# Neighbouring weight rows per partition, an expert's first chunk ahead of the second product before it, and the last merge by high and low parts

## The chip, the cores and the metric

One core of a Trainium2 chip runs the whole program. The metric is the device time of one execution in microseconds (us). The core's engines run side by side: TensorE (PE, with its weight loads as PEld), VectorE (DVE), ScalarE (ACT), GpSimd (POOL) and SyncE (SP, which here only issues DMAs and reads register values). They meet through semaphores. Sixteen DMA engines move data between HBM and the on-chip memory SBUF; products accumulate in PSUM.

## The reference

A backbone of two layers on 512 latent tokens and 256 context tokens of 1024 channels, all fp32. Each layer is a mixer (normalised and modulated input, one combined input projection, a convolution group and a gated recurrent group, an output projection onto the residual) and then a mixture of experts. The part that the change touches is the mixture, per token:

```python
group = top-1 of 4 groups (router logits)
e1, e2, g1, g2 = top-2 of the group's 8 experts, with gates     # 32 experts in all
a, u = split(h @ w_e_gu[e])          # [1024] x [1024, 1024]
y    = (silu(a) * u) @ w_e_down[e]   # [512]  x [512, 1024]
x   += m5 * (g1 * y[e1] + g2 * y[e2])
```

The expert weights are 6 MiB each, 32 experts, two layers: 384 MiB that have to be read once. Layer 1 needs only the 512 latent tokens, since nothing reads the context after it.

## The kernel before

The class `Backbone` builds the program. Each layer runs its mixer, its output projection, the routing (`route`, from L875) and then `moe` (L1419). Routing sorts the experts by their number of tokens; each rank is given a fixed room of rows, and `order` (L1568) lists the ranks in the order in which they are computed, so that big experts stand between small ones. A room is cut by `units` into blocks of 128, 64 or 32 rows ("kinds"). What doesn't fit goes to extra blocks (`overflow`, L1454), which are skipped at run time when there are none. Three experts (7, 8, 9, the "static" ones) are taken ahead of routing, so that their weights can be loaded earlier.

**Weights.** `load_chunks` (L1150 to 1163) loads an expert by chunks of 1 MiB, each 256 rows of 1024 columns: four for the first product (`w_e_gu`), two for the second (`w_e_down`). The chunk lies in SBUF as [128 partitions, 2 x 1024]. At L1161 the source is rearranged as `"a (k p) f -> p (a k) f"`: partition p gets row p and row 128 + p, two runs of 4 KB. The chunks go into a ring of some 16 slots (2.7 experts); SP issues each load, in the order of the program, once the slot's last reader is done.

**A block.** `gather` (L1188) fetches the block's token rows by an indirect DMA on POOL's queue. Blocks of 64 and 32 rows hold the halves and quarters of their rows side by side in the 128 partitions. `rows_in` transposes 128 x 128 pieces on TensorE (L1205), and DVE copies them out of PSUM (xT, L1207). `gate_up` multiplies by the chunks of `w_e_gu` (L1220 for 128 rows, L1224 for 64 and 32, where parts of the columns take the array's column tiles in turn). `activate` copies the result on ACT (L1244), transposes it on TensorE (L1247), and forms silu times the other half on ACT (L1250) and DVE (L1251, L1252): that is hT. Then comes the second product with the two chunks of `w_e_down`: `down` in layer 0 (L1277 for 128 rows, L1289 for others; scaled by DVE at L1291 and scattered to HBM by L1180) and `down_here` in layer 1 (L1315, L1327), where the results stay on chip: DVE multiplies them by gate and modulation (L1329) into a tile YB.

**The merge of layer 1.** Blocks of one kind fill the 128 partitions of a YB tile. When a group is full, `tokens` writes one-hots OT of its tokens (L1349) and `merge` (L1352) multiplies OT by YB in fp32 and adds the products to the residual X (L1371): for each of four token tiles, 1024 columns in products of up to 512 columns. There are 13 merges. After the last one, `finish` normalises and stores the result (L1547 to L1550).

**Order.** `begin` (L1373) is a block's whole first product, chunk by chunk; `end` (L1392) its activation and second product. `moe` runs, for each expert, load, begin, end. SP follows the program's order; the other engines' order is set when the program is built, by a scheduler that goes by priorities and by the buffers that are free. The PSUM buffers are three of the tag "acc", two "pS", one "pA"; those of one tag are taken in the order of the program.

Of the kernel before, what the change touches and what calls it, by code (L numbers as in the profile page):

```python
# [19 lines left out]
D = 1024  # L20
# [13 lines left out]
class Backbone:  # L34
# [3 lines left out]
    # ---------------------------------------------------------------- set-up  # L38
    def setup(self, consts, tmp, ps, dram, stp):
# [34 lines left out]
        # lower bounds of layer 1: softmax over the two layers, exp(x) = s(x) / s(-x) for x <= 0  # L74
# [17 lines left out]
        # masks of the levels inside a diagonal block of 32: [s (4 blocks), level, t]  # L92
# [13 lines left out]
    def setup_router(self, consts, tmp):  # L106
# [21 lines left out]
        # token less 1024 as a multiple of 32 and the rest  # L128
# [19 lines left out]
        # which half or quarter of a row a partition takes, with the index that means no row  # L148
# [8 lines left out]
        # rows over which a static expert counts, and what breaks ties between the counts  # L157
# [12 lines left out]
        # of each rank: first column of the table and one, room, whole blocks of 64 in the room  # L170
# [27 lines left out]
    # ------------------------------------------------------- adaLN modulation  # L198
    def ada_step(self, l, g, k, st, pool, ps, q, bufs):
        # rows of four n-blocks of 512 columns in the four column tiles; k-block k of the contraction  # L200
# [22 lines left out]
        if g == 2:  # L223
            # the second norm's weight times (1 + scale)
            nc.vector.scalar_tensor_tensor(row[:64], row[:64], 1.0, st["nw"], op0=OP.add, op1=OP.mult)
# [11 lines left out]
    def ada_cols(self, l):  # L237
        # per-channel factor of the normalised input, norm weight times (1 + scale), for both streams
        nc = self.nc
        A = self.modA[l]  # L240
        nc.vector.tensor_scalar_add(A, self.modc[l][1], 1.0)
        nc.vector.tensor_mul(A, A, self.nwcol(l, 0).unsqueeze(2).to_broadcast([128, 8, 2]))

    # ---------------------------------------------------------------- mixer
# [7 lines left out]
    def square(self, x, pool):  # L252
        # reciprocal root mean square of each token, and space for the normalised tokens
# [10 lines left out]
    def modulated(self, l, i, H, src, pool):  # L264
        # high and low parts of token tile i of the transposed input from its normalised transpose
# [19 lines left out]
    def norm_first(self, H, pool, ps):  # L285
        # the first layer's input: normalised and transposed while the modulation is still being loaded
# [15 lines left out]
    def norm_next(self, sq, x, pool, ps):  # L302
        # a token tile of a later layer's input, normalised and transposed
# [8 lines left out]
    def split_w(self, src, pool, nat=False, eng=None):  # L312
        # src [1024, 128] in DRAM -> [128, (high, low), 8, 128], or [256, 512] -> [128, (high, low), 2, 512]
# [11 lines left out]
    def proj_T(self, W, H, ps, ctx=True):  # L325
        # transposed projection of 128 features: (PSUM tile, token range) for each half of the tokens
# [10 lines left out]
    def proj_N(self, W, H, i, ps, group=range(4)):  # L337
        # natural product of token tile i with 512 columns, over the k-pairs in group
# [10 lines left out]
    def gates(self, l, hd, pz, t, d, K2, Dk):  # L349
        # forget factors and keys of one direction from the raw gate  # L350
# [16 lines left out]
    def head(self, l, hd, K2, Q2, Dk, q, Vn, SG, pool, hg, ps):  # L367
        """One head of the recurrent group. The decay products of both directions come by halving: at block size b
        the two blocks of a pair meet through products inside each block, so nothing is ever divided."""
# [48 lines left out]
        # blocks of 64, and the pairs of 64 inside 128  # L418
# [28 lines left out]
        # pairs of 128  # L447
# [12 lines left out]
        # pairs of 256 of the latent tokens  # L460
# [8 lines left out]
        # final states of the context, both directions  # L469
# [15 lines left out]
        # outputs, natural  # L485
# [22 lines left out]
    def conv(self, l, cb, H, YC, CS, wcol, pool, wp, ps):  # L508
        # gated short convolution of 128 channels: horizontal for the first half of the channels, else vertical
# [39 lines left out]
    def squares(self, CS, ps):  # L549
        # sums over the channels of the last block's squares, for each token  # L550
# [14 lines left out]
    def mixer(self, l, ps, st, ms):  # L565
# [10 lines left out]
        with pool("hy", "right") as hy, pool("wp", "right") as wp, pool("sg", "right") as sgp:  # L576
# [16 lines left out]
            with pool("p0", "right") as p0:  # L593
# [10 lines left out]
                else:  # L604
                    W = nat(6, range(2), nc.vector)
                    # the token tiles in stages, one behind the other
# [1107 lines left out]
```

## Time and profile before

| | us |
|---|---|
| median of 3 runs (2028.06 to 2033.73) | 2029.3 |
| span of the profiled execution | 2028.5 |
| TensorE busy in it | 1726.0 (85%) |
| DVE busy | 908.2 (45%) |
| ACT busy | 442.2 (22%) |
| POOL busy | 360.8 (18%) |

HBM reads are 530.95 MB, 270 GB/s over the span; of 190665 DMA packets 183720 are under 8 KB. Layer 0's mixture lies from about 560 to 1110 us and layer 1's from about 1500 us to the end. The busy shares are means over stages with different limits, so the stages have to be read one by one: the windows (busy time by engine in a stretch, with the granted clock of TensorE and the DMA's busy share and rate), then what an engine waits for, then the timeline of single instructions. In a timeline line, the first number is the start, the second the duration of the group, "x16" its instructions, and the bracket the idle time of the engine before it with what ended it.

### The profile page before, as it was taken

Reading aid. Unit: us, or ns where it says so; the run is one execution under the profiler, and the core shown is the slowest. Engines: PE = TensorE matmul, PEld = TensorE weight load, DVE = VectorE, ACT = ScalarE, POOL = GpSimd, SP = SyncE. Lnnn points to the kernel's source line nnn. Section 1 sums busy time; section 2 is a strip of 40 time slices with the busy share of each in tenths; the row PEclk is TensorE's granted clock in tenths of the full one; section 3 lists DMA queues with packets and bytes.
Section 4 is the critical chain, followed back from the end, with each engine's and each line's share of the span. In section 5 each row is a group of like instructions: output and inputs, shape, how many; then the busy total and the mean of one; then the engine's idle time right before and its main releaser. Section 6 shows DMA issues by size and latency. Waiting matters only on the chain. (4 is left out here: it accounts for less than half of the span.)

```text
span 2028.5 us, 33494 instructions
## 1 busy us (share of the span) xinstructions
PE 1726.0 (85%) x13488; PEld 1104.1 (54%) x13488; DVE 908.2 (45%) x2141; ACT 442.2 (22%) x871; POOL 360.8 (18%) x282
## 2 busy tenths in 40 slices
PE   5999899999967888888875899889968888888886
PEld 2766778898843343333322688767754434434343
DVE  4425355635664132222222636666564434435344
ACT  3512223323212122111111533333320000000001
POOL 1501221121122111111110632222211000000000
PEclk8999899999988999989998899999988999999998
DMA  7376552262489988999998322114379979999996
GB/s 271 99 266 209 177 201 82 75 238 81 172 316 378 409 323 345 408 408 407 407 408 318 134 85 62 42 53 168 126 291 352 407 297 407 407 402 391 401 407 262
DMA packets 190665, 542.36 MB, mean 267 GB/s; under 512 B 17393, under 2 KB 66719, under 8 KB 183720
## 3 DMA queue, kind: packets, MB, share of 16 engines
q1 hardware_dynamic: 167304, 466.17, 60.0%
q10 hardware_dynamic: 15040, 55.08, 7.9%
q0 software_dynamic: 8160, 18.90, 2.5%
q8 instruction: 108, 1.77, 0.4%
q14 instruction: 53, 0.43, 0.1%
HBM read 530.95 MB, written 15.96 MB: 270 GB/s over the span
## 5 line engine op out<-in xcount | busy, mean ns | idle before, releaser
L1224 PE MATMUL acc<-w,xT 128*32 128x256 f32 (+1 forms) x3360 | 348.4, 449 | 18.3 <-DVE xT L1207 9.8
L1224 PEld LDWEIGHTS acc<-w,xT 128*32 128x32 f32 (+1 forms) x3360 | 137.3, 120 | 221.0 <-issue 152.8
L322 POOL TENSOR_TENSOR hilo<-raw,hilo 128x1024 fp32r<-128x1024 f32 x64 | 157.4, 2465 | 447.9 <-ACT hilo L319 406.7
L333 PE MATMUL acc<-HA,hilo 128*128 128x384 f32 (+1 forms) x960 | 208.0, 359 | 0.0
L333 PE MATMUL acc<-HB,hilo 128*128 128x384 f32 (+1 forms) x960 | 205.4, 357 | 0.0
L1244 ACT COPY au<-acc 128x256 f32<-128x256 f32 (+1 forms) x69 | 31.1, 452 | 718.9 <-PE acc L1224 676.7
L333 PEld LDWEIGHTS acc<-HA,hilo 128*128 128x128 f32 x960 | 171.0, 192 | 16.4 <-issue 4.2
L333 PEld LDWEIGHTS acc<-HB,hilo 128*128 128x128 f32 x960 | 173.7, 193 | 9.5 <-issue 0.8
L1188 POOL DMA_INDIRECT xb<-h,idx x63 | 65.3, 1036 | 533.3 <-PE pS L1205 495.0
L1289 PE MATMUL acc<-w,hT 128*32 128x256 f32 (+1 forms) x816 | 115.1, 542 | 47.0 <-DVE hT L1252 42.4
L345 PE MATMUL acc<-hilo,HA 128*128 128x512 f32 x504 | 133.0, 416 | 11.8 <-POOL HA L283 5.8
L345 PE MATMUL acc<-hilo,HB 128*128 128x512 f32 x504 | 125.7, 397 | 4.6 <-DVE hilo L322 3.3
L1268 DVE SCALAR_TENSOR_TENSOR au<-w,gt,au 32x256 f32<-32x256 f32 (+2 forms) x102 | 58.6, 577 | 148.7 <-ACT au L1267 146.2
L345 PEld LDWEIGHTS acc<-hilo,HA 128*128 128x128 f32 x504 | 99.0, 201 | 40.7 <-POOL HA L283 7.3
L1327 PE MATMUL acc<-w,hT 128*32 128x256 f32 (+1 forms) x896 | 88.5, 440 | 28.5 <-DVE hT L1252 22.4
L319 ACT CAST hilo<-raw 128x1024 fp32r<-128x1024 f32 x80 | 83.5, 1049 | 124.8 <-PE acc L345 40.8
L345 PEld LDWEIGHTS acc<-hilo,HB 128*128 128x128 f32 x504 | 94.3, 190 | 30.0 <-DVE hilo L322 4.4
L389 DVE TENSOR_TENSOR Q<-Q,Dk 128x256 f32<-128x256 f32 (+1 forms) x144 | 89.7, 651 | 27.5 <-PE pA L464 11.8
L1289 PEld LDWEIGHTS acc<-w,hT 128*32 128x32 f32 (+1 forms) x816 | 40.1, 140 | 108.8 <-issue 52.3
L1180 POOL DMA_INDIRECT yb<-ys,idx x39 | 38.9, 998 | 288.6 <-DVE ys L1291 204.4
L1207 DVE COPY xT<-pS 128x256 f32<-128x256 f32 (+1 forms) x79 | 42.5, 541 | 95.9 <-PE pS L1205 82.0
L384 DVE TENSOR_TENSOR K<-K,Dk 128x768 f32<-128x768 f32 x64 | 72.9, 1139 | 24.1 <-ACT tmp L401 21.1
(369 smaller groups left out, 2173.4 us busy)
## 6 DMA issues: line engine op xcount, KB each, us to landing
w<-in_w_e_gu SPq DMA_DIRECT2D x242, 1024.0 KB
w<-in_w_e_down SPq DMA_DIRECT2D x121, 1024.0 KB
adaw<-in_w_ada ACTq DMA_DIRECT2D x40, 1024.0 KB
raw<-in_w_in SPq DMA_DIRECT2D x64, 512.0 KB
adaw<-in_w_ada SPq DMA_DIRECT2D x8, 1024.0 KB
raw<-in_w_out SPq DMA_DIRECT2D x16, 512.0 KB
HA<-in_w_e_gu SPq DMA_DIRECT2D x6, 1024.0 KB
h<-SG SPq DMA_DIRECT2D x10, 512.0 KB
```

Of the source, the lines that this page charges most:

```text
L319: nc.scalar.copy(W[:, 0], w)
L322: eng.tensor_sub(W[:, 1], w, W[:, 0].bitcast(F32))
L333: nc.tensor.matmul(o, W[:, wi, k, :], H[k // 4][:, k % 4, hi, t], start=k == 0 and wi == hi, stop=k == 7 and wi == 1)
L345: nc.tensor.matmul(pa, H[k // 4][:, k % 4, hi, t], W[k // 2][:, wi, k % 2, :], start=k == ks[0] and wi == hi, stop=k == ks[-1] and hi == 1)
L384: nc.vector.tensor_tensor(half(Kv, TOK, 0, kn, b), half(Kv, TOK, 0, kn, b), vw(Dv, b, [[2 * b, n], [TOK - b, 2], [0, b]]), op=OP.mult)
L389: nc.vector.tensor_tensor(o, o, vw(Dv, (TOK + b) * d, [[2 * b, qn // (2 * b)], [0, b]]), op=OP.mult)
L1188: self.nc.gpsimd.indirect_dma_start(out=xb, out_offset=None, in_=rows, in_offset=bass.IndirectOffsetOnAxis(ap=idx, axis=0), bounds_check=r ...
L1207: nc.vector.tensor_copy(t[:, :n].rearrange("p a b -> p (a b)"), pt[:, :128 * n])
L1224: nc.tensor.matmul(pg[kind * u:kind * u + kind, :w], xT[k], gu[:, k % 2, w * u:w * u + w], start=st, stop=sp)
L1268: nc.vector.scalar_tensor_tensor(ms[pr, :o], self.m5s[pr, 0, c], g0[pr], ms[pr, :o], op0=OP.mult, op1=OP.add)
L1289: nc.tensor.matmul(py[kind * u:kind * u + kind, :w], hT[k], dn[k // 2][:, k % 2, w * u:w * u + w], start=k == 0, stop=k == 3)
L1327: nc.tensor.matmul(py[pr, :w], hT[k], dn[k // 2][:, k % 2, c], start=k == 0, stop=k == 3)
```

## The change

- `load_chunks` gives each partition two neighbouring rows, one run of 8 KB. Row 2p and 2p + 1 of a chunk then lie in partition p, so the transposes read every second column (`every_other`) to bring the other operand into the same order.
- `begin` is cut in two: `start` (gather, transposes, the first product with chunk 0) and the rest (chunks 1 to 3). `end` runs the next expert's `start` between the last activation and the last second product, where `ahead` allows it: in layer 1 where the next expert is a single block of fewer than 128 rows, in layer 0 for all but rank 0; never for the last expert. The last static expert takes part.
- The merge of layer 1 splits YB into a high part in fp32r (ACT) and a low part in fp32r (POOL), by halves of 512 columns; each product becomes two fp32r products that add up in PSUM. OT becomes fp32r. OT and the parts YR are new tiles, YB moves into free space of X.
- `overflow` gives back the list of scatters that it found, where before it left an empty one.
- The space kept for DMA descriptors of GpSimd is set to 8192.

The rest of the diff takes comments away. Its core:

```diff
     def load_chunks(self, e, which, tiles, q=None):
...
-            o = (q or self.nc.sync).dma_start(w, src[i, r:r + 256, :].rearrange("a (k p) f -> p (a k) f", p=128))
+            o = (q or self.nc.sync).dma_start(w, src[i, r:r + 256, :].rearrange("a (p k) f -> p (a k) f", p=128))
...
+    def every_other(self, t, j):
+        c = 256 * (j // 2) + j % 2
+        return t[:, c:c + 255:2]
...
-                nc.tensor.transpose(pt[:, 128 * j:128 * j + 128], xb[:, 128 * (a + j):128 * (a + j) + 128], self.ident)
+                nc.tensor.transpose(pt[:, 128 * j:128 * j + 128], self.every_other(xb, a + j), self.ident)
...
-            nc.tensor.transpose(pt[:, 128 * j:128 * j + 128], au[:, 128 * j:128 * j + 128], self.ident)
+            nc.tensor.transpose(pt[:, 128 * j:128 * j + 128], self.every_other(au, j), self.ident)
...
     def merge(self, kind, ps):
...
+        YR = self.YR
+        for h in range(2):
+            c = slice(512 * h, 512 * h + 512)
+            nc.scalar.copy(YR[:, 0, c], YB[:, c])
+            nc.gpsimd.tensor_sub(YR[:, 1, c], YB[:, c], YR[:, 0, c].bitcast(F32))
...
-                nc.tensor.matmul(pa[c // 512][:, c % 512:c % 512 + n], self.OT[:, c // w, 128 * i:128 * i + 128],
-                                 YB[:, c:c + n], start=True, stop=True)
+                for v in range(2):
+                    nc.tensor.matmul(pa[c // 512][:, c % 512:c % 512 + n], self.OT[:, c // w, 128 * i:128 * i + 128],
+                                     YR[:, v, c:c + n], start=v == 0, stop=v == 1)
...
     def begin(self, w, units, xp, ps):
+        b, rest = self.start(w, units, xp, ps)
+        rest()
+        return b
+
+    def start(self, w, units, xp, ps):
...
-        for c in range(4):
-            for j, u in enumerate(units):
-                self.gate_up(u[0], xT[j], c, w[c], pg[j])
-        return w, units, pg
+        def chunks(cs):
+            for c in cs:
+                for j, u in enumerate(units):
+                    self.gate_up(u[0], xT[j], c, w[c], pg[j])
+
+        chunks((0,))
+        return (w, units, pg), lambda: chunks((1, 2, 3))
+
+    def ahead(self, l, units):
+        if l:
+            return len(units) == 1 and units[0][0] < 128
+        return sum(1 if u[0] < 128 else 2 * (j > 0) for j, u in enumerate(units)) < 3
+
+    def end(self, b, pool, ps, last=False, between=None):
         w, units, pg = b
...
             if j + 1 < len(units):
                 hT.append(act(j + 1))
+            elif between is not None:
+                between()
             self.down(kind, hT[j], w[4:], wi, pool, ps, last)
...
-                self.YB.append(mp.tile([128, D], F32, name=f"YB{i}"))
+                self.YB.append(self.X[:, 4 + i, :])
...
-            self.OT = self.X[:, 4:6, :].rearrange("p a (b t) -> p (a b) t", b=2)
+            self.OT = mp.tile([128, 4, 512], F32R, name="OT")
+            self.YR = mp.tile([128, 2, D], F32R, name="YR")
...
-        for n, r in enumerate(self.order[l]):
-            e = nc.sync.value_load(self.eid[0:1, r:r + 1], min_val=32 * l, max_val=32 * l + 31)
-            w = self.load_expert(e, self.ring())
-            if n == 28:
-                self.overflow(l, xp, mp, ps, ms2)
-            self.end(self.begin(w, self.units(l, r), xp, ps), mp, ps, n == 28)
-            if l:
-                for u in self.units(l, r):
+        for b in stat[:-1]:
+            self.end(b, mp, ps)
+        cur = stat[-1]
+        for n in range(-1, N):
+            nxt = []
+            fits = n + 1 < N - 1 and self.ahead(l, self.units(l, order[n + 1]))
+            self.end(cur, mp, ps, n == N - 1, (lambda: nxt.append(begin(n + 1))) if fits else None)
+            if l and n >= 0:
+                for u in self.units(l, order[n]):
                     left.remove(u[0])
                 flush()
+            if n + 1 == N - 1:
+                load(n + 1)
+                self.overflow(l, xp, mp, ps, ms2)
+            if n + 1 < N:
+                cur, rest = nxt[0] if nxt else begin(n + 1)
+                rest()
```

Here `load(n)` reads the expert's number and issues its six loads once, and `begin(n)` calls it and then `start`.

## Rows read from the trace of the kernel before

**Rows 1.** Windows by stage: us, busy us (instructions) of each engine, PEclk, DMA share, GB/s.

```profile
260.00:263.00 3.00, 3.00 (x19) 3.00 (x18) 0.00 (x0) 0.00 (x0) 0.00 (x0) 1.00 1.01 423
417.00:435.00 18.00, 18.00 (x101) 18.00 (x101) 5.51 (x67) 3.89 (x6) 3.04 (x2) 0.91 1.02 418
624.00:796.00 172.00, 152.06 (x868) 64.35 (x868) 47.39 (x89) 29.84 (x57) 27.34 (x28) 0.95 0.92 362
796.00:1074.00 278.00, 227.76 (x1706) 92.12 (x1698) 77.00 (x156) 55.74 (x110) 43.35 (x43) 0.92 1.03 407
1559.00:1662.00 103.00, 90.00 (x534) 40.67 (x534) 45.05 (x125) 4.97 (x12) 4.99 (x5) 0.97 0.90 356
1662.00:1990.00 328.00, 280.03 (x2372) 132.23 (x2376) 139.16 (x375) 19.10 (x50) 22.95 (x23) 0.98 1.02 402
1990.00:2004.00 14.00, 8.40 (x113) 4.20 (x106) 7.55 (x39) 1.02 (x3) 0.00 (x0) 0.88 1.00 397
```

**Rows 2.** Waits of TensorE, 796 to 1073 us: total us, times, longest us.

```profile
PE acc L1289 <- DVE hT L1252: 25.0, 12, 2.6
PE pS L1247 <- ACT au L1244: 9.3, 15, 0.7
```

**Rows 3.** Timeline of TensorE, 1073 to 1084 us: start, us, instruction, [idle before].

```profile
1074.55 1.94 PE L1224 MATMUL acc<-w,xT 128*64 128x512 f32 x8 [1.41 <-DMA w<-in_w_e_gu]
```

**Rows 4.** Waits of TensorE, 1662 to 1990 us.

```profile
PE acc L1327 <- DVE hT L1252: 17.9, 15, 1.4
```

**Rows 5.** DMA packets, 260 to 263 us.

```profile
DMA packets 171, 1.27 MB, mean 423 GB/s; under 512 B 16, under 2 KB 16, under 8 KB 16
```

**Rows 6.** Line 410 by form: min/median/max ns, first and last start.

```profile
L410 PE MATMUL pS<-Q,tmp x1600: 189/196/260, 169.1 to 1379.4; 128*32 128x32 f32 x178
...
L410 PE MATMUL pS<-q,tmp x320: 192/196/217, 167.8 to 1363.0; 128*32 128x32 f32 x160
```

**Rows 7.** Timeline of TensorE, 636 to 680 us.

```profile
639.06 5.34 PE L1289 MATMUL acc<-w,hT 128*64 128x512 f32 x16 [2.55 <-DVE hT L1252]
644.33 3.66 PE L1224 MATMUL acc<-w,xT 128*32 128x256 f32 x64
...
653.13 7.09 PE L1224 MATMUL acc<-w,xT 128*64 128x512 f32 x32
660.96 0.66 PE L1247 MATMUL pS<-ident,au 128*128 128x128 f32 x4 [0.74 <-ACT au L1244]
...
664.38 6.32 PE L1289 MATMUL acc<-w,hT 128*64 128x512 f32 x16 [2.55 <-DVE hT L1252]
```

**Rows 8.** Waits of TensorE, 624 to 796 us.

```profile
PE acc L1289 <- DVE hT L1252: 12.5, 6, 2.6
...
PE acc L1224 <- DVE xT L1207: 1.5, 2, 0.8
```

**Rows 9.** Timeline, 1952 to 1964 us, a merge.

```profile
1952.36 1.88 PE L1367 MATMUL pA<-YB,X 128*128 128x512 f32 x4
...
1954.28 1.29 DVE L1371 TENSOR_TENSOR X<-pA,X 128x512 f32<-128x512 f32 x2 [0.17 <-PE pA L1367]
```

**Rows 10.** Timeline, 1993 to 2029 us, the last merge.

```profile
2008.14 1.07 PE L1327 MATMUL acc<-w,hT 128*32 128x256 f32 x16
...
2009.82 0.70 PE L1367 MATMUL pA<-xw,X 128*128 128x256 f32 x2 [0.62 <-DVE xw L1329]
...
2012.09 1.89 PE L1367 MATMUL acc<-xw,X 128*128 128x256 f32 x8
```

**Rows 11.** Timeline of TensorE near 271 and 499 us: fp32r products.

```profile
271.81 2.24 PE L333 MATMUL acc<-HB,hilo 128*128 128x384 f32 x12
...
498.71 21.02 PE L345 MATMUL acc<-hilo,HA 128*128 128x512 f32 x92
```

**Rows 12.** Lines 282 and 283 by form: min/median/max ns.

```profile
L282 ACT CAST HB<-mod x6: 614/617/622, 1130.8 to 1159.4; 128x512 fp32r<-128x512 f32 x6
...
L283 POOL TENSOR_TENSOR HB<-mod,HB x12: 1280/1290/2255, 50.9 to 1160.8; 128x512 fp32r<-128x512 f32 x12
```

More of the change, by code (lines that the diff above doesn't have):

```diff
@@ L1237, in activate @@
             for j in range(4):
-                nc.tensor.transpose(pt[:, 128 * j:128 * j + 128], h[:, 128 * j:128 * j + 128], self.ident)
+                nc.tensor.transpose(pt[:, 128 * j:128 * j + 128], self.every_other(h, j), self.ident)
             nc.scalar.copy(hT.rearrange("p a b -> p (a b)"), pt)
@@ L1386, in begin @@
                 pg.append([ps.tile([128, 512], F32, name="acc", bufs=3) for _ in range(2)])
-        for c in range(4):
-            for j, u in enumerate(units):
-                self.gate_up(u[0], xT[j], c, w[c], pg[j])
-        return w, units, pg
-    def end(self, b, pool, ps, last=False):
+        def chunks(cs):
[9 more added lines that the diff above has]
+    def end(self, b, pool, ps, last=False, between=None):
         w, units, pg = b
@@ L1425, in moe @@
             for i in range(2):
-                self.YB.append(mp.tile([128, D], F32, name=f"YB{i}"))
+                self.YB.append(self.X[:, 4 + i, :])
                 nc.gpsimd.memset(self.YB[-1], 0.0)
-            self.OT = self.X[:, 4:6, :].rearrange("p a (b t) -> p (a b) t", b=2)
+            self.OT = mp.tile([128, 4, 512], F32R, name="OT")
+            self.YR = mp.tile([128, 2, D], F32R, name="YR")
             self.groups, self.into = {}, {}
-        for b in stat:
-            self.end(b, mp, ps)
         left = [u[0] for r in self.order[l] for u in self.units(l, r)]
@@ L1439, in flush, with load, begin @@
                     self.merge(kind, ps)
-        for n, r in enumerate(self.order[l]):
-            e = nc.sync.value_load(self.eid[0:1, r:r + 1], min_val=32 * l, max_val=32 * l + 31)
-            w = self.load_expert(e, self.ring())
-            if n == 28:
-                self.overflow(l, xp, mp, ps, ms2)
-            self.end(self.begin(w, self.units(l, r), xp, ps), mp, ps, n == 28)
-            if l:
-                for u in self.units(l, r):
+        order = self.order[l]
+        ws = {}
+        def load(n):
+            if n not in ws:
+                r = order[n]
+                e = nc.sync.value_load(self.eid[0:1, r:r + 1], min_val=32 * l, max_val=32 * l + 31)
+                ws[n] = self.load_expert(e, self.ring())
+        def begin(n):
+            load(n)
+            return self.start(ws[n], self.units(l, order[n]), xp, ps)
+        N = len(order)
+        for b in stat[:-1]:
[7 more added lines that the diff above has]
+                for u in self.units(l, order[n]):
                     left.remove(u[0])
                 flush()
+            if n + 1 == N - 1:
[4 more added lines that the diff above has]
+                rest()
     def overflow(self, l, xp, mp, ps, ms2):
@@ L1456, in overflow @@
         NOV = self.NOV
+        scats = self.scats
         _, vals = nc.values_load_multi_w_load_instructions(self.nov[0:1, 0:1], min_val=0, max_val=NOV)
@@ L1522, in overflow @@
                     self.merge(64, ps)
-        self.scats = []
+        self.scats = scats
     def combine(self, l, i, cp):
@@ L1701 @@
     from concourse.bass_utils import run_bass_kernel_spmd as _run
-    nc = _bacc.Bacc("TRN2", target_bir_lowering=False, num_devices=1)
+    nc = _bacc.Bacc("TRN2", target_bir_lowering=False, num_devices=1, dynamic_dma_scratch_size=8192)
     arrays, io = {}, {}
```

## The prediction

> **What bounds the kernel now.** I read the windows by stage first, then what TensorE waits for, then its timeline at single boundaries between experts, and last the end of the run. The two layers' expert stages are nearly all weight traffic: from 796 us to 1074 us and from 1662 us to 1990 us the DMA engines show a busy share above 1 and a flat 407 and 402 GB/s [rows 1]. In a stretch like that the end is set by two things only: when the stretch began, and the rate. Each stretch begins where TensorE has caught up enough to free the ring of weight chunks: ahead of them the mean is 362 GB/s (624 to 796 us) and 356 GB/s (1559 to 1662 us) [rows 1], because the big experts there occupy TensorE longer than their weights take to load. So the kernel is bound twice over, first by TensorE and then by DMA.
>
> It isn't DMA alone, though. In 796 to 1073 us TensorE never waits for a weight; it waits 25.0 us in 12 places for the activation of its own first product, and 9.3 us in 15 places for the copy ahead of it [rows 2]. It runs into weights that have not landed only at 1074.55 us [rows 3]. The TensorE chain, its own gaps included, is as long as the transfers. **A faster transfer therefore pays only if that chain becomes shorter too, and the reverse**; both are touched here. In layer 1 it is alike: 17.9 us in 15 waits for the activation [rows 4]. The profiled span is 2028.5 us and the median 2029.3 us, 0.8 us above it; I sum against the span and add the 0.8 at the end.
>
> **Part 1, one run of 8 KB per partition instead of two of 4 KB.** It touches the 32 x 6 chunks of 1 MiB of each layer, at line 1161. The price is the rate per full busy share. 4 KB loads with little else beside them moved 418 GB/s at a share of 1.02, so 410; the adaLN weights, whose rows give 8 KB runs (155 of the 171 packets are not under 8 KB [rows 5]), moved 423 at 1.01, so 419 [rows 1]. That is 2.2%. The lower end is the plain ratio, 423 to 418 or 1.2%. The upper end is against the ring's own stretch, 402 in place of 423 or 5.2%; it counts the short gather packets of those stretches as if the change removed them, so I stay near the like-for-like row and take 2.6%, a little above it, since the ring's packets take longer than those. The saturated stretches are 796 to 1082 us and 1662 to 2003 us, 286 and 341 us: 2.6% is **7.4 and 8.9 us** (3.4 to 14.9 and 4.1 to 17.7).
>
> By the Trainium skill ("DMA: Bandwidth & Descriptors", section "Why small descriptors are slow (HBM only)") a packet carries a fixed overhead of about 3 cycles beside one per 32 bytes, and joining packets is worth it only at 256 bytes or less. As an estimate from that page, 131 cycles twice against 259 is 1.15%, 7 us for both layers in place of 16; the ratio of the rows goes above that, and no run of before moves expert weights in 8 KB runs.
>
> **Part 2, transposes that read every second column.** The number and size of the transposes stays; only the stride of what they read changes. The nearest pair are the small products of one head, with a plain and with a strided operand: median 196 ns both, 106 to 113 ns for the weight load both [rows 6]. I put it at 0; four transposes take 0.66 us [rows 7], so if the stride cost a tenth, the 380 would cost 6 us, the other end.
>
> **Part 3, the next expert's chunk 0 ahead of the second product.** At a boundary TensorE ends the first product, transposes, and stands until DVE has made hT: 2.55 us at 639.06 and at 664.38 us [rows 7]. A quarter of the next first product now fits there: 0.9 us for a block of 32 rows (64 instructions in 3.66 us), 1.8 us for one of 64 (32 in 7.09 us) [rows 7]. In 624 to 796 us there are six such waits, 12.5 us together, and two for xT, 1.5 us [rows 8]. One of the six stands before rank 0 and isn't filled. The rest take 0.9 three times, and 1.8 twice, and the xT waits go: 2.7 + 3.6 + 1.5 = 7.8 us. The second product after a gap is also slow: 5.34 and 6.32 us [rows 7] where 16 at the pace of 32 in 7.09 us [rows 7] would be 3.55, so 1.8 and 2.8 lost to the lower of the two clock levels. I count half of that, 2.3 us. Sum **10 us** (3 if only the waits before 32-row experts go, 14 if every wait listed does). It moves the start of the saturated stretch, and so the end of layer 0, one for one. Inside that stretch the chain gains 12 boundaries at 0.9 to 1.8 us, some 16 us, against the 7.4 that the faster weights ask of it; so both move together. In layer 1 the same in 1559 to 1662 us: five boundaries, one of 1.8 and four of 0.9, 5.4 us. Inside the saturated stretch, 15 waits of 17.9 us [rows 4] give back some 13, enough for 8.9. Of what moves with it: the gather of the next block, one DMA on POOL's queue, is asked for earlier on a queue with slack; the weight loads on SP keep their order, and each waits as before for its slot.
>
> **Part 4, the last layer's merge.** Before, a merge of a 64- or 128-row group is 16 instructions of 512 columns (four in 1.88 us [rows 9]), one of a 32-row group 32 of 256 (eight in 1.89 us [rows 10]): 7.5 us either way, two passes for each fp32 product. After, the two passes are fp32r products: 92 of 512 columns took 21.02 us, 0.23 each, and twelve of 384 took 2.24, 0.19 each [rows 11]; the weight loads set that pace, so I take it for 256 too. 16 x 0.23 = 3.7 us, 32 x 0.19 = 6.0 us: 3.8 and 1.5 less. New is a lead-in: for each half ACT writes the high part (0.62 us) and POOL the low part (1.29 us in the median, 2.26 at most) [rows 12]. The first half is ready after 1.9 us, the second after 3.2. Then DVE's eight additions, 0.64 us each (two in 1.29 [rows 9]), are the floor, 5.2 us in all: the last additions end some 0.6 + 2 x 1.3 + 0.5 + 6 x 0.65 = 7.6 us after the group is full, where the products alone took 7.5 before. Unfilled a merge is thus about the same length (up to -1.3, lost); filled with the next expert's chunks up to +2. Waiting behind POOL's subtractions on its queue are only gathers that are asked for early, and ACT's copies stand ahead of an activation by 0.6 us. I take 0 for the merges inside the stretch, and -1.4 in all for the three ahead of 1662 us, which leaves **4 us** of the 5.4. At the very end nothing fills it: the last merge now begins 0.62 us after the first scaling [rows 10] and chases the others; behind the parts it can't. **-1.6** (to -2.8).
>
> **The rest.** The weights of layer 1 come at 397 GB/s until 2004 us [rows 1], and the last second product uses the last of them at 2008.14 [rows 10], about 4 us later; a chain shortened by part 3 takes that back: **+4** (0 if it isn't). Scatters no longer ordered behind the overflow's, and the smaller descriptor space: 0, as nothing waits for them.
>
> **Sum.** Layer 0: 10 + 7.4 = 17.4. Layer 1: 4 + 8.9 + 4 - 1.6 = 15.3. 2028.5 - 32.7 + 0.8 = **1997 us**, rounded up.
>
> **The rivals.** (a) *The longer packets bring only 1.2%*, the plain ratio of [rows 1]: 627 us x 1.2% = 7.5 in place of 16.3, **2004 us**. The Trainium skill's rule on packets would give about the same. (b) *The rate stays*, since the bound of a saturated stretch is elsewhere than in the packets: only 10 + 4 - 1.6 and the 4 at the end remain, **2013 us**. Against it stands that two kinds of stretch, both saturated, differ in rate [rows 1]. (c) *The chain isn't shortened*: the order of the engines puts chunk 0 behind the second product, as the accumulators in use block it, or the lower clock stays; then TensorE is the bound of both stretches and the faster weights are hidden: 3 us at most, **2025 us**. For it: TensorE runs into missing weights only at 1074.55 [rows 3]. (d) *Slower: the merge's lead-in.* If POOL's subtractions take their longest, 2.26 us [rows 12], a merge ends 0.6 + 4.5 + 0.5 + 3.9 = 9.5 us after its group is full in place of 7.5 and a little, and DVE's scaling of the next block stands behind its additions: with 2.7 us at 13 merges, 35 us, against the 18 that part 3 gives back in layer 1, and 1.6 at the tail, layer 1 gets 19 us longer; layer 0 gains 10 (one of its two parts): **2038 us**. It decides from the point where the lead-in is longer than the TensorE work that stands ready beside it. Against it: the median of 1.29 [rows 12], and that chunks of the next expert can stand there.
>
> **How the numbers follow.** Forecast 0.55, by itself 1981 to 2009. (a) 0.15, (b) 0.08, (c) 0.11, (d) 0.11. Adding the ends of the unknown costs (all waits closed and 5.2% gives 1977 or so), the range that holds eight in ten reaches from 1977 to 2022. A measurement of this kernel tells about 0.3%, 6 us, from no change; so faster is the forecast, (a) and (b), 0.78; (c) is mostly within, 0.10; (d) is slower, 0.12.
>
> **What would show it.** After: the queue of the weights has some 49 thousand packets fewer, and 98 thousand fewer are under 8 KB; 418 to 420 GB/s in the saturated stretches; groups of 8 or 16 first products ahead of a second product in TensorE's timeline, with waits for hT nearly gone; the stretch of layer 0 starts near 786 us; TensorE waits for weights earlier than 1074 us; each merge behind a copy on ACT and a subtraction on POOL. If the rate stays below 410, part 1 is wrong; if the second products still follow idle time of 2 us, part 3 is; if the merges idle TensorE by more than 3 us each, (d) holds.

## The result, and the profile after

| | us |
|---|---|
| before, median in the first comparison (2028.06 to 2033.73, 4 runs) | 2030.97 |
| changed, median (1996.05 to 2005.23, 4 runs) | 1998.14 |
| ratio, with its 95% interval | 0.9844 (0.9822 to 0.9865) |
| changed, median in a second comparison (5 runs; before 2029.48, 11 runs) | 1998.96 |
| its ratio | 0.9843 (0.9815 to 0.9870) |
| span of the profiled execution, before and after | 2028.5 and 1994.8 |

The forecast was 1997 us. The page of the changed kernel counts the packets:

```profile
DMA packets 141513, 542.35 MB, mean 272 GB/s; under 512 B 17394, under 2 KB 66720, under 8 KB 85417
```

That is 49152 packets fewer in all and 98303 fewer under 8 KB (183720 before): 384 chunks, each with 128 packets in place of 256. The stages of the changed kernel by windows (columns as in [rows 1]); the first two lines are layer 0's saturated stretch and its end, the other two layer 1's:

```profile
784.00:1052.00 268.00, 223.93 (x1622) 93.65 (x1622) 74.80 (x155) 54.41 (x108) 42.89 (x41) 0.93 1.01 417
1052.00:1068.00 16.00, 11.55 (x70) 4.20 (x72) 2.77 (x5) 2.41 (x4) 0.99 (x1) 0.82 1.01 418
...
1636.00:1950.00 314.00, 266.90 (x2346) 127.39 (x2338) 146.04 (x386) 30.25 (x68) 45.80 (x41) 0.98 1.01 416
1950.00:1960.00 10.00, 4.19 (x52) 1.88 (x52) 3.60 (x19) 0.65 (x2) 0.00 (x0) 1.00 1.02 419
```

The rate is 417 and 416 GB/s where it was 407 and 402 [rows 1]. TensorE's waits show whose turn it is now, first in layer 0 ahead of the saturated stretch (610 to 784 us, which answers to [rows 8]):

```profile
PE acc L1230 <- DVE xT L1213: 6.5, 7, 1.5
...
PE acc L1295 <- DVE hT L1258: 1.7, 1, 1.7
```

and then inside it (784 to 1056 us, which answers to [rows 2]):

```profile
PE acc L1230 <- DMA w<-in_w_e_gu: 14.3, 5, 5.5
```

The waits for hT have all but gone, from 12.5 us to 1.7 us and from 25.0 us to nothing, and TensorE waits for weights: 14.3 us, where it waited for none before. The transfers alone are the bound there now. What took the place of a wait for hT is a wait for xT, the next block's own rows. The timeline of TensorE, to be held against [rows 7]:

```profile
626.05 0.75 PE L1253 MATMUL pS<-ident,au 128*128 128x128 f32 x4 [0.69 <-ACT au L1250]
626.64 0.40 PE L1211 MATMUL pS<-ident,xb 128*128 128x128 f32 x2
627.91 1.07 PE L1230 MATMUL acc<-w,xT 128*32 128x256 f32 x16 [0.87 <-DVE xT L1213]
629.69 3.65 PE L1295 MATMUL acc<-w,hT 128*64 128x512 f32 x16 [0.71 <-issue]
...
639.11 3.00 PE L1230 MATMUL acc<-w,xT 128*64 128x512 f32 x8 [1.51 <-DVE xT L1213]
642.05 2.50 PE L1295 MATMUL acc<-w,hT 128*32 128x256 f32 x32
```

Ahead of the second product at 629.69 us stand 1.07 us of the next expert's chunk 0, but they begin 0.87 us late, since DVE ends a scaling first and copies xT, from 627.44 us, among the steps of hT. At 639.11 us the wait for xT is 1.51 us, eight instructions take 3.00 us where the warm pace is 1.94 [rows 3], and the second product behind them 2.50 where 1.93 is warm.

### The profile page after: what moved, and what is told of

Its sections match the earlier page's. It is cut to its first block, busy times and chain, and to the rows that moved or that the text cites. A ratio compares the mean times of both kernels' runs of the same rounds, so it can differ in the third digit from the quotient of the medians.

```text
span 1994.8 us, 33498 instructions
## 1 busy us (share of the span) xinstructions
PE 1700.2 (85%) x13488; PEld 1098.2 (55%) x13488; DVE 914.0 (46%) x2141; ACT 458.2 (23%) x897; POOL 394.3 (20%) x308
## 5 line engine op out<-in xcount | busy, mean ns | idle before, releaser
L1230 PE MATMUL acc<-w,xT 128*32 128x256 f32 (+1 forms) x3360 | 378.4, 454 | 59.1 <-DVE xT L1213 34.6
L345 PEld LDWEIGHTS acc<-hilo,HB 128*128 128x128 f32 x504 | 94.5, 190 | 29.1 <-DVE hilo L322 4.5
L1295 PE MATMUL acc<-w,hT 128*32 128x256 f32 (+1 forms) x816 | 97.2, 478 | 12.4 <-DVE hT L1258 6.4
L389 DVE TENSOR_TENSOR Q<-Q,Dk 128x256 f32<-128x256 f32 (+1 forms) x144 | 89.6, 651 | 23.7 <-PE pA L464 11.8
L1333 PE MATMUL acc<-w,hT 128*32 128x256 f32 (+1 forms) x896 | 87.4, 440 | 7.3 <-DVE hT L1258 5.2
L1297 DVE TENSOR_TENSOR ys<-acc,au 128x256 f32<-128x256 f32 (+1 forms) x34 | 18.4, 542 | 124.9 <-PE acc L1295 124.5
```

Source lines behind the costliest of these rows:

```text
L345: nc.tensor.matmul(pa, H[k // 4][:, k % 4, hi, t], W[k // 2][:, wi, k % 2, :], start=k == ks[0] and wi == hi, stop=k == ks[-1] and hi == 1)
L389: nc.vector.tensor_tensor(o, o, vw(Dv, (TOK + b) * d, [[2 * b, qn // (2 * b)], [0, b]]), op=OP.mult)
L1230: nc.tensor.matmul(pg[kind * u:kind * u + kind, :w], xT[k], gu[:, k % 2, w * u:w * u + w], start=st, stop=sp)
L1295: nc.tensor.matmul(py[kind * u:kind * u + kind, :w], hT[k], dn[k // 2][:, k % 2, w * u:w * u + w], start=k == 0, stop=k == 3)
L1333: nc.tensor.matmul(py[pr, :w], hT[k], dn[k // 2][:, k % 2, c], start=k == 0, stop=k == 3)
```

## The experiments

One table for all of them. It is read off the profiles by a ruler that doesn't depend on where a wait is booked: the time at which a given weight chunk had landed, counted back over the bytes of the weight queue. "Start" is from the issue of one given load (in layer 0 the third routed expert's second, in layer 1 the first routed expert's third) to the landing of the chunk that opens the saturated stretch. "Stretch" is 102 chunks in layer 0 and 114 in layer 1, and the chunk that closes it is the fifth and the ninth before the layer's last. "Rest" ends with the layer's last second product, "end" is from there to the end of the span, and "else" is all of the span that is left: mixers, routing, the first experts. Each line adds up to the span of its profile. Every variant is made from the changed kernel and keeps its loop and its `overflow`; `a_alone`, `c_alone` and both `no_d` have the old descriptor space as well, and no run changes that space by itself.

```
us                       layer 0: start stretch  rest   layer 1: start stretch  rest   end    else
before                            181.4   275.8  21.8            153.9   303.1  28.5  19.3  1044.7
a_alone                           181.4   269.7  21.6            155.1   306.7  33.4  19.4  1037.1
c_alone                           176.0   275.5  23.6            153.4   299.1  30.1  19.4  1044.6
d_alone                           180.7   275.7  21.9            152.5   300.1  32.5  20.7  1044.8
no_c                              183.2   269.3  23.2            155.4   302.9  34.0  21.7  1047.0
no_d                              178.6   269.0  23.4            155.5   292.0  29.5  19.4  1043.8
no_d_b                            174.6   269.1  23.5            151.8   292.1  28.9  19.4  1049.4
no_a                              173.2   275.5  23.6            150.7   299.4  29.6  21.0  1044.5
changed, first profile            176.9   269.1  23.2            148.5   292.1  29.1  20.7  1035.2
after_again                       177.7   269.2  23.5            149.5   292.1  29.1  20.7  1043.5
after_b                           174.0   269.3  23.8            148.5   292.1  29.1  20.8  1041.7
plain                             177.1   269.1  22.7            149.4   292.0  29.2  21.0  1044.7
plain_tail                        173.9   268.9  23.4            149.4   292.0  29.2  19.3  1047.1
short_runs                        180.3   291.3  20.7            154.5   318.1  29.2  20.0  1052.0
```

The stretches repeat to within a few tenths of a microsecond wherever the transfers are the bound. The starts scatter by some 4 us, and "else", where no kernel but `plain` and `plain_tail` changes an instruction of the mixers, scatters by more than 10 us. The chunk that bounds a stretch is met to within some half a chunk, so that a start can be 1 to 2 us too long, and its rest as much too short (`a_alone`, `d_alone` and `no_c` above all).

**8 KB runs alone (a_alone).** The kernel before with

```diff
-            ...rearrange("a (k p) f -> p (a k) f", p=128))
+            ...rearrange("a (p k) f -> p (a k) f", p=128))
```

and the transposes to match.

> The kernel before with 8 KB runs and the strided transposes alone. My theory (TensorE's chain is as long as the transfers): the saturated stretches show some 417 GB/s at first, but the ring then runs against TensorE, the mean rate there falls back towards 410, and the time is 0 to 6 us below before (2024 to 2030). Rival (the gains simply add): the rate alone gives its 2.5% over 627 us, 15 us less, about 2015. If the strided transposes cost a tenth each: some 3 us above my theory.

Measured: ratio 1.0009 (0.9984 to 1.0034), median 2030.83 against 2032.38. Nothing is left of 2.4% of the rate. The windows of the two stretches:

```profile
796.00:1070.00 274.00, 225.29 (x1677) 93.83 (x1677) 77.04 (x156) 54.83 (x109) 43.35 (x42) 0.95 1.01 417
1653.00:1976.00 323.00, 277.79 (x2180) 131.50 (x2180) 134.22 (x356) 18.43 (x48) 22.95 (x23) 0.96 0.98 399
```

In layer 0 the rate is there, 417 GB/s, and the stretch is 6.1 us shorter. In layer 1 the DMA share falls to 0.98 and the rate to 399: the ring waits for TensorE, and the stretch and the rest behind it are 3.6 and 4.9 us longer. So the gain of one layer is lost in the other. That TensorE is late there shows at the end: by the bytes of the queue, the last weights had landed 11.3 us before the last second product ended in `a_alone` and 11.8 us in `no_c`, and 3.2 us in before. TensorE's mean granted clock differs with it: 0.95 and 0.96 in the two stretches here, 0.92 and 0.98 before [rows 1]. Where TensorE is the bound, such dips are time; what makes them differ is open. `no_c`, which has the new merge as well, shows the same.

**Chunk 0 ahead, alone (c_alone).** The changed kernel with the runs of 4 KB, plain transposes and the fp32 merge, in effect the kernel before with `start`, `end`, `ahead` and the new `overflow`.

> The kernel before with the next expert's chunk 0 ahead of the second product alone; runs of 4 KB, the old merge. My theory: the saturated stretches start 5 to 10 us earlier in each layer, their rate stays 407 GB/s, TensorE waits for weights before their end: 10 to 16 us below before (2014 to 2020). Rival (the chain isn't what counts, the rate is): within 4 us of before.

Measured: ratio 0.9948 (0.9929 to 0.9967), median 2023.07: 9 to 11 us less, at the lower end of what I expected. Windows of the stretches, and what TensorE waits for in the second one:

```profile
788.00:1060.00 272.00, 221.35 (x1621) 89.19 (x1621) 72.23 (x148) 53.38 (x106) 43.31 (x41) 0.92 1.03 407
1659.00:1980.00 321.00, 280.80 (x2311) 128.13 (x2308) 138.14 (x364) 19.00 (x50) 22.95 (x23) 0.99 1.03 407
```

```profile
PE acc L1229 <- DMA w<-in_w_e_gu: 7.3, 3, 5.5
```

The rate is that of 4 KB runs, 407 GB/s, and now in both layers; before, layer 1 had 402. The 114 chunks take 299.1 us in place of 303.1: before, TensorE had held up the transfers of layer 1 by 4 us, unseen, since the share stood at 1.02. Layer 0's stretch starts 5.4 us earlier, layer 1's only 0.5, where I had expected 5 to 10 us in each.

**The merge alone (d_alone).** The changed kernel with `return False` in `ahead`, 4 KB runs and plain transposes.

> The kernel before with the merge by high and low parts alone. My theory: the lead-in of copy and subtraction eats what the cheaper products save, so within 4 us of before (2026 to 2034). Rival (the lead-in is unfilled at each of 13 merges, 2 to 3 us each): 10 us or more above before. Rival on the other side (the merge is what moved layer 1's stretch by 9 us in the changed kernel): 6 to 9 us below before.

Measured: ratio 0.9988 (0.9968 to 1.0008). No change that can be told, as my theory said; the end is 1.4 us longer, and the rest of layer 1 by 4.0, against 4.4 less ahead of it.

**Without chunk 0 (no_c).** The changed kernel with

```diff
     def ahead(self, l, units):
+        return False
```

> The changed kernel without chunk 0 ahead (8 KB runs and the new merge stay). My theory: near the time of 8 KB runs alone, 2020 to 2030, as the chain binds. Rival (gains add): 2012 or less.

Measured: ratio 0.9992 (0.9972 to 1.0011). The runs of 8 KB and the merge together are worth nothing that can be told without the chunk ahead. By the medians the parts alone give 1.6, 9.3 and 1.9 us, 13 us, of which only the 9.3 is clear of the scatter; the whole is 31 to 33 us. The difference is what the parts give each other. For the merge it can be read from TensorE's waits for the two parts, over the whole run; here:

```profile
PE pA L1379 <- ACT YR L1369: 20.6, 13, 1.8
PE pA L1379 <- POOL YR L1370: 9.3, 13, 0.9
```

and in the changed kernel:

```profile
PE pA L1379 <- POOL YR L1370: 9.7, 17, 0.9
PE pA L1379 <- ACT YR L1369: 7.0, 7, 1.8
```

That is 2.3 us a merge without chunk 0 ahead and 1.3 us with it.

**Without the merge (no_d, no_d_b).** The changed kernel with

```diff
-                for v in range(2):
-                    nc.tensor.matmul(..., self.OT[...], YR[:, v, c:c + n], start=v == 0, stop=v == 1)
+                nc.tensor.matmul(..., self.OT[...], YB[:, c:c + n], start=True, stop=True)
```

OT and YB where they were before, and the descriptor space as before.

> The changed kernel with the old fp32 merge. My theory (the merge is worth about nothing in the stretch and costs 2 us at the end): 1995 to 2000, the same as the changed kernel. Rival (the cheaper products are what let the chain of layer 1 keep up): 2004 or more.

Measured: ratio 0.9891 (0.9859 to 0.9923), median 2009.98: not what I expected, and what the rival said. It was run again beside the changed kernel on one chip:

> The changed kernel with the old fp32 merge again, beside the changed kernel. The profiles so far put the new merge's worth at 6 to 7 us in layer 1's stretch with chunk 0 ahead, less 1.4 us at the end: 4 to 7 us above the changed kernel. If that was the scatter of single runs: the same within 2 us.

Measured: ratio 0.9891 (0.9862 to 0.9920) and median 2009.6, where the changed kernel (`after_b`) has 0.9843 and 1998.96. The medians are 10.6 us apart, and both runs of `no_d` agree. The stages account for a part: layer 1's start is 151.8 and 155.5 us here, 148.5 to 149.5 in the changed kernel, so 2 to 7 us, less 1.4 at the end. The rest of the difference lies in "else" in these profiles (1049.4 against 1041.7), where the two kernels differ only in the space kept for descriptors and in where YB and OT lie; why the medians keep it is open, and a part of the 10.6 us may belong to that and not to the merge. How the merge pays is seen at the 128-row group, one of three ahead of layer 1's stretch. TensorE's timeline without the new merge (no_d_b):

```profile
1633.41 7.13 PE L1321 MATMUL acc<-w,hT 128*128 128x512 f32 x16 [0.43 <-ACT hT L1245]
1640.38 1.02 PE L1373 MATMUL pA<-xw,X 128*128 128x512 f32 x2
...
1646.38 1.02 PE L1373 MATMUL acc<-xw,X 128*128 128x512 f32 x2
...
1649.74 1.91 PE L1333 MATMUL acc<-w,hT 128*32 128x256 f32 x32
```

and with it (after_b):

```profile
1624.11 7.13 PE L1321 MATMUL acc<-w,hT 128*128 128x512 f32 x16 [0.43 <-ACT hT L1245]
1630.68 1.02 PE L1379 MATMUL pA<-YR,OT 128*128 128x512 f32 x2
...
1633.15 0.50 PE L1379 MATMUL pA<-YR,OT 128*128 128x512 f32 x1 [0.75 <-ACT YR L1369]
...
1635.07 0.50 PE L1379 MATMUL pA<-YR,OT 128*128 128x512 f32 x1 [0.72 <-POOL YR L1370]
...
1636.18 1.48 PE L1230 MATMUL acc<-w,xT 128*32 128x256 f32 x18
...
1638.72 1.93 PE L1333 MATMUL acc<-w,hT 128*32 128x256 f32 x32
```

From the second product of the block (L1321) to that of the next one it is 16.3 us without and 14.6 us with the new merge. The lead-in does stall TensorE (0.75 us for ACT, 0.72 us for POOL), but the first half is split and multiplied while the block's second product still runs (630.68 lies within it: 1624.11 + 7.13 is 1631.24), and 18 products of the next expert stand between the merge's products at 1636.18.

**4 KB runs (no_a).** The changed kernel with the old rearrangement and plain transposes.

> The changed kernel with runs of 4 KB and plain transposes. My theory: the starts of the saturated stretches stay 6 to 9 us earlier, their rate falls back to 407 GB/s: 2012 to 2018. If the packets were worth nothing: 1998.

Measured: ratio 0.9936 (0.9911 to 0.9961), median 2018.26 against 2030.19, at the upper end of what I expected. With chunk 0 ahead, the runs of 8 KB shorten the stretches by 6.3 and 7.3 us (275.5 to 269.2, 299.4 to 292.1); that is 13.6 of the 19 us by which the ratios of this run and of the changed kernel differ, and for the rest the stages show no single place. Without chunk 0 ahead the long runs were worth nothing.

**2 KB runs (short_runs).** As `no_a`, and each chunk by two DMAs of 512 columns:

```diff
+            for h in range(2):
+                s = slice(512 * h, 512 * h + 512)
+                o = (q or self.nc.sync).dma_start(w[:, :, s], src[i, r:r + 256, s].rearrange("a (k p) f -> p (a k) f", p=128))
```

> The changed kernel with each chunk loaded by two DMAs of 512 columns, so runs of 2 KB. If a packet has a fixed cost, read from 408 GB/s at 4 KB and 418 at 8 KB as 2.4% of an 8 KB packet's time, 2 KB runs move about 389 GB/s in the saturated stretches, and the time is some 30 us above the version with 4 KB runs, 2040 to 2050. Rival (what counts is that a partition reads two neighbouring rows, not the packets' number): 405 to 410 GB/s as with 4 KB.

Measured: ratio 1.0176 (1.0133 to 1.0219), median 2067.41, 49 us above `no_a` where I had expected some 30. Windows of the two stretches:

```profile
810.00:1090.00 280.00, 227.33 (x1517) 92.28 (x1516) 68.59 (x140) 50.50 (x98) 41.17 (x39) 0.92 1.05 386
1690.00:2020.00 330.00, 284.84 (x2200) 124.18 (x2200) 138.96 (x357) 29.64 (x66) 44.85 (x40) 0.97 1.04 383
```

386 and 383 GB/s, a little below the 389 that a fixed price gives. Per chunk, the 102 of layer 0 take 2.64 us by 8 KB runs, 2.70 by 4 KB and 2.86 by 2 KB. Each of the 16 engines moves 8, 16 and 32 packets of a chunk: 0.062 us for 8 more packets and 0.155 us for 16 more, **7.7 and 9.7 ns a packet** (8.0 and 10.3 by the 114 chunks of layer 1). So the time goes with the number of packets, at a price that is fixed to within a third, and neighbouring rows alone don't explain it. The runs of 2 KB come with twice as many DMAs too, and no run separates the two. The stretches are 15.8 and 18.7 us longer than in `no_a`; the rest of the 49 us lies in the starts (7.1 and 3.8) and in "else".

**The changed kernel again (after_again, after_b).**

> The changed kernel once more, for a second profile. In the first the layer 0 mixer, whose instructions and their order are those of before, was 9 us shorter than in the profile of before. If that belongs to the change, it is 9 us shorter here too; if executions differ by that, it lies anywhere between.

> The changed kernel beside the next three, on one chip. 0.984 to 0.989 of before. Its profile is also a third look at the stages: the expert stages 469 to 471 us in each layer, the mixers anywhere within some 10 us.

Measured: 2007.07 us (one run) and 1998.96 us. "Else" is 1035.2, 1043.5 and 1041.7 us in the three profiles, 1037 to 1052 in the others and 1044.7 in that of before. So the first weight load, at 402.4 us in the first profile and 411.6 us in that of before, tells nothing about the change: 9.5 us of the 33.7 us between those two profiles lie in "else", and nearly all of it (9.2 us) ahead of that load, where the instructions are the same.

**Plain transposes (plain, plain_tail).** The columns are put in order where they are written, for instance

```diff
-        nc.scalar.copy(au[:, :w], pg[:, :w])
+        nc.scalar.copy(self.flat(au[:, :w]), self.swap(pg[:, :w]))
```

(`flat` and `swap` are views of 256 columns as two runs of 128, and as 128 pairs); `plain_tail` also computes the very last merge from YB in fp32.

> The changed kernel with the columns put in order where they are written (the normalised tokens by DVE, the first product's copy by ACT, and the router's weights to match), so that the transposes read neighbouring columns again. In the changed kernel four transposes take 0.75 us in place of 0.66. My theory: some 9 us of TensorE go, but most of it under the transfers, so 0 to 4 us below the changed kernel, in the parts ahead of the saturated stretches. Rival (the cost only moves, as the copy reads with a stride): 0 to 4 us above it.

> As the one before, and the very last merge by fp32 products without the parts: the stretch from the last second product to the end is 19.4 us in place of 20.7, and all else the same, so 1 to 1.5 us below it.

Measured: ratios 0.9846 (0.9819 to 0.9874) and 0.9857 (0.9829 to 0.9884), medians 1999.37 and 2001.16, beside 1998.96 of the changed kernel. The transposes did get shorter; the xb transposes by form (minimum, median, maximum in ns), in the changed kernel and in `plain`:

```profile
L1211 PE MATMUL pS<-ident,xb x190: 270/283/489, 582.6 to 1963.6; 128*128 128x128 f32 x190
```

```profile
L1222 PE MATMUL pS<-ident,xb x190: 270/273/477, 582.8 to 1970.1; 128*128 128x128 f32 x190
```

283 and 273 ns, but the stages don't move by more than they scatter: where the transfers are the bound, TensorE's 10 ns don't count, and in the starts they are less than the scatter. The fp32 merge at the very end does take 1.5 us off the end (19.3 in place of 20.8), and that can't be told from no change in the time. No version here beats the changed kernel.

## Why the prediction was right, step by step

The time was right, 1997 forecast and 1998 measured, but that it is right to a microsecond is luck. The main reasons held: the kernel was bound by TensorE's chain and by DMA at once, neither part pays without the other, and the transfers alone are the bound afterwards. Single terms were off, and errors of several us cancelled. Before against `after_b`, whose span is 29.2 us shorter:

| step | forecast | before to after_b | what the runs show |
|---|---|---|---|
| layer 0, start (chunk 0 ahead) | -10 | -7.4 | -3.7 to -7.4 in three profiles, -5.4 in c_alone |
| layer 0, rate | -7.4 | -6.5 | 2.4%, the same in all |
| layer 0, rest | 0 | +2.0 | +1.4 to +2.0 in the three profiles, +1.4 in no_c too |
| layer 1, start | -4 | -5.4 | -4.4 to -5.4; with the merge left out only +1.6 to -2.1 |
| layer 1, stretch (rate) | -8.9 | -11.0 | 7.0 to 7.3 by the packets, 3.7 to 4.0 by transfers that TensorE no longer holds up |
| layer 1, rest | -4 | +0.6 | nothing is taken back |
| end (lead-in of the last merge) | +1.6 | +1.5 | 0.7 to 2.4 with the new merge |
| all else | 0 | -3.0 | scatter, -9.5 and -1.2 in the other two profiles |

**The rate** was the surest step and came out: 2.6% forecast from the adaLN rows, 2.4 to 2.5% measured. The rule of the Trainium skill that I had put against it ("DMA: Bandwidth & Descriptors", section "Why small descriptors are slow (HBM only)") says that joining packets pays only at 256 bytes or less, and an estimate from it gives 1.15%; the traces show twice that at 4 KB. Another figure of the same page of the Trainium skill lies nearer: its section "Measured (HBM→SBUF, 128 partitions, SWDGE, issued from GpSimd)" gives the least time of a small load as 64 packets of about 10.5 ns each. Here a packet more costs 7.7 to 10.3 ns; these loads are issued by SP, and no run here shows that the two are the same cost.

**The start of layer 0** was mis-sized, 10 for 3.7 to 7.4. I let chunk 0 fit into the whole wait for hT. It has a wait of its own: xT comes through the same DVE, between the steps of hT. In the stretch ahead, TensorE's waits for hT and xT together went from 14.0 us [rows 8] to 8.2 us, not to nothing. And what was won came mostly by another term, the clock. The same work can be set side by side, from the second product at 639.06 us [rows 7] to one at 790.05 us before, and from 629.69 to 776.18 us in the first profile after. The windows, all of TensorE and then its second products alone, before:

```profile
639.06:790.05 150.99, 136.14 (x747) 0.94 0.93 368
639.06:790.05 150.99, 26.16 (x177) 8.75 (x177) 0.94 0.93 368
```

and after:

```profile
629.69:776.18 146.49, 133.78 (x748) 0.98 0.93 379
629.69:776.18 146.49, 20.33 (x176) 7.70 (x176) 0.98 0.93 379
```

Of the 4.5 us, TensorE's idle time gave only 2.1 (14.9 to 12.7), where I had 7.8. The second products gave 5.8, where I had 2.3: those at 629.69 and 654.23 us take 3.65 us each at a granted clock of 1.00, where the ones in [rows 7] took 5.34 and 6.32 at 0.68 and 0.57. Two terms went the other way. The first products take 1.7 us more, mostly since the lower level now meets the ones behind the pause of 1.51 us (3.00 us at 639.11); and the transposes, which I had at 0, take 2.0 us more (11.0 to 13.0). The other two profiles show the same: idle time 2.9 and 2.0 us less, second products 5.5 and 7.3 us less.

**The 4 us at the end of layer 1** were no slack. Between the landing of the last chunk of the first product and the last second product lie an activation and a second product whatever the transfers do, so "landed 4 us before it is used" is a latency, not a reserve: from the landing that closes the stretch, nine chunks before the last, to the end of the last second product it is 28.5 us before, and 29.1 after. The reading was off too: by the bytes of the queue the last weights landed at 2006.1 us, not 2004, and 3.2 us before that end; after it is 2.5 us. The step failed because I compared a landing with a use without asking which chunk the chain behind it had waited for. The 3.7 to 4.0 us that the stretch itself gave back, by transfers no longer held up, took its place in the sum by chance; no step of mine had it.

**The rest of layer 0** got longer, which I had at 0. The bound has moved to the transfers, so TensorE comes late to the end of layer 0, and at a granted clock of 0.82 (1052 to 1068 us above). Its timeline in the first profile:

```profile
1053.23 3.42 PE L1230 MATMUL acc<-w,xT 128*64 128x512 f32 x8 [5.55 <-DMA w<-in_w_e_gu]
1056.59 1.93 PE L1295 MATMUL acc<-w,hT 128*32 128x256 f32 x32
...
1067.79 6.39 PE L1295 MATMUL acc<-w,hT 128*64 128x512 f32 x16 [2.47 <-DVE hT L1258]
```

It stands 5.55 us at chunk 0, with the second product of the expert before it ready behind it, and the last product of 16 takes 6.39 us, where it took 5.35 us in the profile of before, and 3.55 us is warm:

```profile
1088.37 5.35 PE L1289 MATMUL acc<-w,hT 128*64 128x512 f32 x16 [2.57 <-DVE hT L1252]
```

**The merge** has two halves. At the end of the run my step held. The timeline of the last merge, all engines:

```profile
1972.97 1.07 PE L1333 MATMUL acc<-w,hT 128*32 128x256 f32 x16
1974.11 1.98 DVE L1335 SCALAR_TENSOR_TENSOR xw<-acc,gt,m 32x256 f32<-32x256 f32 x4 [4.03 <-PE acc L1333]
1975.21 0.62 ACT L1369 CAST YR<-xw 128x512 fp32r<-128x512 f32 x1 [5.78 <-DVE xw L1335]
...
1975.91 2.50 POOL L1370 TENSOR_TENSOR YR<-xw,YR 128x512 fp32r<-128x512 f32 x2 [41.89 <-ACT YR L1369]
...
1977.23 0.62 PE L1379 MATMUL pA<-YR,OT 128*128 128x256 f32 x3 [0.85 <-POOL YR L1370]
```

It starts behind a copy and a subtraction, as forecast, and the end is 1.5 us longer. Ahead of layer 1's stretch I had it as a loss of 1.4 us; there it is a gain of 2 to 7 in layer 1's start (with what the descriptor space may have in it), as the low and high parts go by halves and the next expert's products fill the lead-in, which is my upper end (+2 a merge) and not the middle. The products themselves are cheaper than I had them, too: for 256 columns I took 0.19 us, by the pace of the weight loads, and eight take 1.11 us, 0.14 each:

```profile
1981.48 1.11 PE L1379 MATMUL pA<-YR,OT 128*128 128x256 f32 x8
```

POOL took 1.27 us for each half in every merge, and TensorE waited 1.3 us a merge for the parts, so rival (d), which rested on 2.26 us and asked for idle times of over 3 us, had nothing to stand on.

**The rivals.** By the terms of the sum (a) comes to 2005 and (c) to 2026 us, a microsecond above what stands there. (a) is out by the rate, (b) as well. (c), the chain that isn't shortened, is what `a_alone` and `no_c` show: 2031 and 2033 us, where I had 2025. I had taken it to be a case of the order of engines; it is what the 8 KB runs are worth by themselves. The strided transposes, 0 in the sum, cost more than the tenth that I had for the other end (four in 0.75 us at 626.05, 0.66 in [rows 7]); but `plain` shows that taking it away moves no stage by more than the starts' scatter of some 4 us.

Not settled: why TensorE's granted clock is higher in layer 0's stretch and lower in layer 1's in both kernels with 8 KB runs and no chunk 0 ahead (0.95 and 0.96; 0.94 and 0.95 in `no_c`), and what makes the 10 us between the medians of `no_d` and the changed kernel, of which the stages of layer 1 show 1 to 6.

## What to carry to other kernels

Where a transfer runs at full share and the engine that consumes it never waits for it, the two may be of equal length: a faster transfer alone may bring nothing, and the work that shortens the engine's chain is worth more with it than without. Each packet saved was worth some 8 to 10 ns here even at 4 KB, which counts only where hundreds of megabytes pass through. And compare stages, not spans: here more than a quarter of the difference between two profiles lay in stages whose instructions were the same. Where a gap is filled, look also at the products behind it: here more was won by their running at the higher clock level than by the gap itself.

## What the runs showed of the hardware

- A DMA share above 1 doesn't prove that the transfers run unhindered: in layer 1 before, 1.02 and 402 GB/s stood beside some 4 us of transfers held up (303.1 us for chunks that take 299.1 to 299.4 as soon as TensorE keeps up).
- TensorE's transposes of fp32 take 283 ns in place of 273 with every second column read, and their weight loads 209 ns in place of 140 (medians of 190, `after_b` and `plain`). The same 76 of them ahead of layer 0's stretch take 12.5 us in place of 11.2, both at a granted clock of 1.00 (`after_b` and `plain_tail`).
- With 8 KB runs and no chunk 0 ahead, TensorE's mean granted clock over layer 1's stretch was 0.96 (`a_alone`) and 0.95 (`no_c`), where before had 0.98 [rows 1].
- A second product of the same 16 instructions took 3.65 us at a mean granted clock of 1.00 (after, 629.69 us), 5.34 us at 0.68 and 6.32 us at 0.57 behind a pause of 2.55 us (before, 639.06 and 664.38 us).
